# A key transpose placed later in the gate's product, and layer results stored from ScalarE's queue

## The chip, the cores and the metric

One Trainium2 chip, one of its cores. The metric is the device time of one execution in microseconds (us); lower is better. The kernel is built with a tile framework: the program emits instructions, a scheduler orders them on each engine, and helper calls force an order where the author wants one.

## The reference

One layer of a bidirectional encoder is applied to two request groups (prompt and sample), each 2048 tokens of width 1024, in fp32, with shared weights:

```python
h = rms_norm(x, norm_w)
q_a, k_a, v_a, g_a, q_b, k_b, v_b, g_b = split(h @ w_in)      # 512 128 128 512 512 512 512 512
q_a, k_a = rope(rms_norm(q_a)), rope(rms_norm(k_a))            # 8 query heads, 2 key heads of 64
o_a = windowed_gqa_sink(q_a, k_a, v_a, sink_a) * silu(g_a)     # +-128 tokens
o_b = neighbourhood_attn(rms_norm(q_b), rms_norm(k_b), v_b, rpb_b) * silu(g_b)   # 2-D window 8 x 16
x = x + concat([o_a, o_b]) @ w_out
y = x + (p @ w_ple) * sigmoid(x @ w_ple_gate)                  # p: 256 wide per token
```

## The kernel before

Every large product is done in fp32 precision by splitting both operands into a high and a low part and adding three matmuls for each block of 128 rows of the contraction: high by high, high by low, low by high.

**The start.** `proj_a(f)` makes group A's projections for one tile of 128 tokens (f = 0 to 31, two groups of 16 tiles): 24 matmuls of `pk` (keys and values), 24 of `pq` (queries), 24 of `pg` (gates), each 24 being 8 blocks k by 3. The first two tiles run interleaved while the weights still arrive: pk for both, pq for both, then pg of tile 0 and pg of tile 1. The gate's weights `wb` are split into their parts by ACT (L151) and DVE (L152) while PE already runs. The keys are normalised on DVE, rotated by POOL (L520 writes `kt`), and turned by a transpose on PE in `keys_a` (`pkt`, through the helper at L255), from which ACT and DVE write the two parts of the key matrix `ks_a`. `keys_a` is called behind matmul number `ka` of the run pq-then-pg; `KA = 33` means behind the tenth matmul of pg. Later PE needs the rotated query `q` in the same way (`pqt`).

**The middle.** Group B's projections follow (`proj_b`, `pqk` and `pvg`), interleaved with the attention units: a unit is one block of queries. `unit_b` loads its values `vw` (three tiles of 256 KB, L865), computes scores `scb`, a softmax, transposes the probabilities (`ptb`), copies them into a high part on ACT (`p_t`, L894) and a low part on DVE (L895), and multiplies them with `vw` (`pob`; one matmul for each of the unit's three blocks of keys, so each needs its own `vw`). The next unit's queries are prepared in between: ACT writes `q1b` (L836), DVE `q` (L837), twice each. A table sets the order of these parts against the filling matmuls.

**The last six units** (about 1735 to 1821 us) have no projections left to fill PE's waits. The filler is `ple_ahead(n)`: the layer's own product `p @ w_ple` of a tile of 512 tokens, in eight pieces m of 128 columns. Each piece takes six matmuls (`pple`), then ACT copies the sum to `ev` (L1003), and a DMA of 256 KB stores it to `ple_d`. A piece is stored on SP's queue (L981) once the next has been copied. `load_coming` loads, also on SP's queue, weights for the last stage into the tiles `wa0` to `wb7` (512 KB each, L972, `sp_oa`). n = 0 to 4 run inside the units; n = 5 to 7 follow with `tail=True` (stored directly, L1006), with nothing else beside them. After that comes the last stage (output projection and gate, `acca` and `accc`, L1225), which reads `ple_d` back.

**Queues.** The program gives every DMA one of eight semaphores in turn, DMAHW0 to DMAHW7, whichever engine issues it. A DMA waits at its place in the engine's queue until the one before it on the same semaphore, eight DMAs earlier in the order of emission, has landed. `P(...)` keeps an instruction in program order on its engine; everything else is ordered by the scheduler.

Of the kernel before, what the change touches and what calls it, by code (L numbers as in the profile page):

```python
# [69 lines left out]
KA = 33  # L70
# [30 lines left out]
def emit(ctx, tc, io):  # L101
    nc = tc.nc
# [4 lines left out]
    def ptile(shape, tag, name):  # L107
        tag = PSM.get(tag, tag)
        return pp.tile(shape, F32, tag=tag, name=name, bufs=PSB[tag])
# [49 lines left out]
    P = tc.keep_in_program_order  # L159
# [6 lines left out]
    def flush(key):  # L166
        pump(max((i + 1 for i, (k, _) in enumerate(jobs) if k == key), default=0))
# [83 lines left out]
    def mm(out, lhsT, rhs, start, stop):  # L251
        pinned(nc.tensor.matmul(out, lhsT, rhs, start=start, stop=stop))  # L252
# [216 lines left out]
    last = {2 * NT - 2: 48, 4 * NT - 2: 24, 6 * NT - 2: 24}  # L469
# [14 lines left out]
    def proj_a(f):  # L484
        s, t = divmod(f, NT)
        xr, ms, (ssq, ee) = xt.pop(f), ms_a[:, f:f + 1], stats.pop(f)
        ka = 22 if f in last else KA
        early = 1 < f < 2 * NT - 1
        pk = ptile([128, 256], "pj" if f > 1 else "sc", "pk")
        for i, c in enumerate(project(pk, xr, lambda k, b: wx[:, k, b, :], 112)):  # L490
# [439 lines left out]
    ple_d = [dram.tile([128, KT, TW], F32, tag=f"ple_d{n}", name=f"ple_d{n}") for n in range(len(tiles))]  # L930
    p_st, p_rs, early = {}, {}, {}

    def load_p(n):
        if n < len(tiles):
            s, u = tiles[n]
            p_st[n] = []
            for k in range(2):
                st = main.tile([128, TW], F32, tag="stage", name="p32", bufs=2)
                nc.sync.dma_start(st, io["p_t"][s][128 * k:128 * k + 128, TW * u:TW * u + TW])
                p_st[n].append(st)  # L940

    def split_p(n, later=False):

        t = p_rs[n] = main.tile([128, 2, 2, TW], F32R, tag="xr", name="p_r", bufs=2)

        def job(hi, lo, src):
            nc.scalar.copy(hi, src)
            nc.vector.tensor_tensor(out=lo, in0=src, in1=hi.bitcast(F32), op=ALU.subtract)
        for k, src in enumerate(p_st.pop(n)):
            todo = partial(job, t[:, k, 0], t[:, k, 1], src)  # L950
            if later:
                jobs.append((f"p{n}", todo))
            else:
                todo()
# [13 lines left out]
    def load_coming(n=1):  # L968

        for name, tag, key in coming[:n]:  # L970
            w = main.tile([128, 2, 512], F32R, tag=tag, name=tag, bufs=1)
            nc.sync.dma_start(w.bitcast(F32), parts_d[key])  # L972
            early[name].append(w)
        del coming[:n]

    made = []

    def store_ple(n):

        for dst, ev in made[:n]:  # L980
            nc.sync.dma_start(dst, ev)  # L981
        del made[:n]

    def ple_ahead(n, tail=False):

        load_p(n + 1)
        for m in range(KT):
            if m % 4 == 3 and (n < 3 or m == 3):
                load_coming()
            ps = ptile([128, TW], "pj", "pple")  # L990
            if m == 5 and n + 1 < len(tiles):
                split_p(n + 1)
            flush("p0")
            for k in range(2):
                w, c = early["p"][2 * (m // 4) + k], 128 * (m % 4)
                for i, (a, b) in enumerate(((0, 0), (0, 1), (1, 0))):
                    mm(ps, w[:, a, c:c + 128], p_rs[n][:, k, b], k == 0 and i == 0, k == 1 and i == 2)
                    yield 215
            if tail:
                ev = main.tile([128, TW], F32, tag="s", name="ev", bufs=SB)  # L1000
            else:
                ev = ap.tile([128, TW], F32, tag=("ev", "sq")[m // 2 % 2], name="ev", bufs=3 - m // 2 % 2)
            P(nc.scalar.copy(ev, ps))  # L1003
            store_ple(1)
            if tail:
                nc.sync.dma_start(ple_d[n][:, m], ev)  # L1006
            else:
                made.append((ple_d[n][:, m], ev))

    qs = {}  # L1010

# [4 lines left out]
    def filler(f):  # L1016

        gen = proj_a(f) if f < 2 * NT else proj_b(f)
        for n, (cost, last_one) in enumerate(gen):
            if last_one:  # L1020
                next(gen)
            elif hold[0] > 0:
                hold[0] -= 1
            elif n % step[0] == step[0] - 1:
                pump()
            yield cost
# [22 lines left out]
    def paired(f, n):  # L1049
# [20 lines left out]
        else:  # L1070
            for name in ("a12", "a22"):
                load_early(name)
        w_b[half] = w

    stream = chain(*(paired(f, last[f]) if f in last else filler(f) for f in range(2, 6 * NT) if f - 1 not in last),
                   *(ple_ahead(n) for n in range(AHEAD)))
    drain(stream, 24)
    done = 2
# [38 lines left out]
    with tc.tile_pool(name="c", bufs=1, reuse_waits="tile") as op:  # L1117
# [171 lines left out]

        load_raw(0, 0)  # L1290
        drain(ple_ahead(AHEAD, True))
        load_raw(0, 1)
        drain(ple_ahead(AHEAD + 1, True))
        for _ in range(4):
            load_x()
# [12 lines left out]
        for m in range(7 * len(groups)):  # L1308
            n, i = divmod(m, 7)
# [92 lines left out]
```

## Time and profile before

| | before |
|---|---|
| median of 3 runs | 2472.81 us (2471.73 to 2474.23) |
| profiled execution, its own time | 2471.11 us |
| span of its profile | 2469.3 us |
| PE (matmuls) busy | 2453.1 us, 99% |
| PEld (weight loads) busy | 2074.2 us, 84% |
| DVE, ACT, POOL busy | 1703.8, 1413.5, 856.4 us |
| granted PE clock | 1.00 |

PE is TensorE, ACT ScalarE, DVE VectorE, POOL GpSimd, SP SyncE, which here only issues DMAs. A row of a timeline gives start, duration, engine, line, operation, output and inputs, and in square brackets the idle time ahead of it with the instruction that ended it; "x24" means so many instructions in one row. ACTq and SPq are the DMA issues of these engines.

### The profile page before, as it was taken

The page shows a single profiled execution, that of the slowest core. Times are in us where ns is not written, and L with a number is a line of the kernel's source. Part 1 is how long each engine was busy: PE and PEld are TensorE (multiplying, and loading weights), DVE is VectorE, ACT ScalarE, POOL GpSimd, SP SyncE. Part 2 cuts the span into 40 slices and gives each one's busy share as a digit, 9 for nine tenths or more (in the row PEclk, how much of TensorE's full clock was granted, in tenths as well). Part 3 has the DMA queues.
Part 4 walks back from the last instruction along what each step waited for, and adds up shares of the span by engine and source line. Part 5 has one row for each costly group of instructions (what it writes and reads, how often), then busy time and mean ns, then how long its engine had stood idle before and what let it go on. Part 6 is the DMA issues. An engine that isn't in the chain of part 4 may idle for free.

```text
span 2469.3 us, 40516 instructions
## 1 busy us (share of the span) xinstructions
PE 2453.1 (99%) x13050; PEld 2074.2 (84%) x13050; DVE 1703.8 (69%) x4212; ACT 1413.5 (57%) x3407; POOL 856.4 (35%) x1363
## 2 busy tenths in 40 slices
PE   9999999999999999999999999999999999999999
PEld 8888888888888888888888888888888888888887
DVE  7777777777765666666666666666537655677776
ACT  7777776777664665656655566665763212344433
POOL 4555555555543544454544444443110000000000
PEclk9999999999999999999999999999999999999999
DMA  6332223232255565556955566567977445756765
GB/s 227 122 103 93 95 88 103 95 101 88 95 180 164 169 191 183 183 163 196 313 183 179 173 218 202 193 202 230 311 251 269 156 166 175 270 180 207 251 222 170
DMA packets 243172, 442.01 MB, mean 179 GB/s; under 512 B 27888, under 2 KB 82320, under 8 KB 237712
## 3 DMA queue, kind: packets, MB, share of 16 engines
q1 hardware_dynamic: 242672, 439.42, 54.4%
q8 instruction: 104, 1.70, 0.3%
q14 instruction: 108, 0.88, 0.1%
q10 hardware_dynamic: 288, 0.01, 0.0%
HBM read 309.29 MB, written 134.23 MB: 180 GB/s over the span
## 4 chain that ended last, share of the span: by engine, by line
PE 93%; DVE 2%; DMA 2%; ACT 2%; POOL 1%; issue 0%; SPq 0%; DVEq 0%; ACTq 0%; POOLq 0%
PE acca L1225 14%; PE pvg L252 14%; PE pqk L252 14%; PE accc L1225 10%; PE pg L252 7%; PE pq L252 6%; PE scb L252 4%; PE ptb L255 3%; PE pob L252 3%; PE pk L252 3%; PE po L252 3%; PE pple L252 3%; PE sc L252 3%; PE pt L255 2%; DMA vw<-v_d 1%; PE pktb L255 1%
## 5 line engine op out<-in xcount | busy, mean ns | idle before, releaser
L284 ACT ACTIVATE s<-s,nm 128x320 f32<-128x320 f32 (+6 forms) x512 | 294.4, 576 | 317.8 <-DVE nm L279 198.5
L252 PE MATMUL pvg<-wb,xr 128*128 128x512 f32 x1536 | 461.8, 407 | 0.0
L252 PE MATMUL pqk<-wa,xr 128*128 128x512 f32 x1536 | 443.0, 411 | 0.0
L252 PEld LDWEIGHTS pqk<-wa,xr 128*128 128x128 f32 x1536 | 266.0, 189 | 37.0
L252 PEld LDWEIGHTS pvg<-wb,xr 128*128 128x128 f32 x1536 | 266.7, 189 | 31.2 <-DMA wb<-sp_1wb 0.4
L1207 ACT CAST opd<-raw 128x512 fp32r<-128x512 f32 x224 | 131.5, 619 | 271.2 <-PE acca L1225 118.6
L353 POOL TENSOR_TENSOR xr<-stx,xr 128x512 fp32r<-128x512 f32 x186 | 238.9, 1294 | 100.8 <-ACT xr L352 76.0
L1208 DVE TENSOR_TENSOR opd<-raw,opd 128x512 fp32r<-128x512 f32 x224 | 146.4, 685 | 146.6 <-ACT opd L1207 146.6
L252 PE MATMUL pg<-wb,xr 128*128 128x512 f32 x768 | 233.2, 409 | 1.0 <-DVE vv L510 1.0
L252 PE MATMUL pq<-wa,xr 128*128 128x512 f32 x768 | 219.3, 400 | 0.0
L268 DVE CUSTOM_DVE_ANT_0 s<-scb,bias 128x288 f32<-128x288 f32 (+3 forms) x256 | 142.0, 555 | 104.8 <-PE scb L252 101.5
L137 POOL TENSOR_TENSOR yb<-vrb,power 128x8 f32<-128x8 f32 x64 | 106.4, 1662 | 222.7 <-DVE vrb L783 197.1
L1225 PE MATMUL accc<-opd,wb 128*128 128x512 f32 x768 | 176.7, 389 | 0.0
L1225 PE MATMUL acca<-opd,wa 128*128 128x512 f32 x768 | 175.5, 389 | 0.0
L1225 PE MATMUL acca<-opd,s 128*128 128x512 f32 x768 | 175.4, 389 | 0.0
L1225 PEld LDWEIGHTS acca<-opd,wa 128*128 128x128 f32 x768 | 144.2, 188 | 29.9
L1225 PEld LDWEIGHTS accc<-opd,wb 128*128 128x128 f32 x768 | 144.2, 188 | 29.9
L1225 PEld LDWEIGHTS acca<-opd,s 128*128 128x128 f32 x768 | 144.2, 188 | 29.9
L914 DVE TENSOR_TENSOR otb<-pob,otb 64x512 f32<-64x512 f32 x128 | 88.1, 689 | 114.0 <-ACT otb L913 112.4
L252 PEld LDWEIGHTS pob<-p_t,vw 128*128 128x128 f32 (+2 forms) x832 | 132.5, 189 | 27.6 <-DVE p_t L895 4.6
L252 PEld LDWEIGHTS pq<-wa,xr 128*128 128x128 f32 x768 | 135.1, 189 | 17.3
L711 DVE TENSOR_TENSOR pr<-pt,pr 128x512 fp32r<-128x512 f32 (+2 forms) x248 | 135.6, 549 | 17.3 <-ACT pr L709 14.1
(168 smaller groups left out, 5166.8 us busy)
## 6 DMA issues: line engine op xcount, KB each, us to landing
stx<-x_b SPq DMA_DIRECT2D x128, 256.0 KB
vw<-v_d SPq DMA_DIRECT2D x112, 256.0 KB
stx<-x_a SPq DMA_DIRECT2D x64, 256.0 KB
stn<-x_n SPq DMA_DIRECT2D x64, 256.0 KB
v_d<-vb SPq DMA_DIRECT2D x64, 256.0 KB
ple_d<-ev SPq DMA_DIRECT2D x64, 256.0 KB
xres<-x_r SPq DMA_DIRECT2D x64, 256.0 KB
x_d<-r SPq DMA_DIRECT2D x64, 256.0 KB
```

Of the source, the lines that this page charges most:

```text
L137: nc.gpsimd.tensor_tensor(out=y, in0=v, in1=power.broadcast_to([128, n]), op=ALU.pow)
L252: pinned(nc.tensor.matmul(out, lhsT, rhs, start=start, stop=stop))
L255: pinned(nc.tensor.transpose(out, in_, eye))
L268: nc.vector.tensor_tensor_reduce(out=s, in0=ps[:, :n], in1=bias, scale=1.0, scalar=-3.0e38, op0=ALU.add, op1=ALU.max, accum_out=sm["mx"][: ...
L284: ex = nc.scalar.activation(ss[i], ss[i], AF.Exp, bias=nm[:, i:i + 1], accum_out=den[:, i:i + 1])
L353: low.tensor_tensor(out=lo, in0=raw, in1=hi.bitcast(F32), op=ALU.subtract)
L711: nc.vector.tensor_tensor(out=pr[r, 1, to], in0=pt[r, c], in1=pr[r, 0, to].bitcast(F32), op=ALU.subtract)
L914: nc.vector.tensor_tensor(out=ot[a:a + 64], in0=pq[a:a + 64], in1=ot[a:a + 64], op=ALU.add)
L1207: P(nc.scalar.copy(hi, v))
L1208: P(nc.vector.tensor_tensor(out=lo, in0=v, in1=hi.bitcast(F32), op=ALU.subtract))
L1225: pinned(nc.tensor.matmul(ps, w[k][:, a, c:c + 128], o[:, b], start=i in (0, 1, 4) and k == 0 and j == 0, stop=k == 3 and j == 2, skip_gro ...
```

## The change

Two things change. The first tile's key transpose is called behind matmul 44 in place of 33 of the run pq-then-pg: behind the 21st matmul of pg, eleven later. And every store of a piece of `ple_d` is issued from ACT's queue, directly behind the copy that makes it, in place of SP's; the list of pieces made but not yet stored goes, and all 64 stores have one form.

```diff
     def proj_a(f):
-        ka = 22 if f in last else KA
+        ka = 22 if f in last else 44 if f == 0 else KA
...
-    made = []
-
-    def store_ple(n):
-
-        for dst, ev in made[:n]:
-            nc.sync.dma_start(dst, ev)
-        del made[:n]
-
     def ple_ahead(n, tail=False):
...
             P(nc.scalar.copy(ev, ps))
-            store_ple(1)
-            if tail:
-                nc.sync.dma_start(ple_d[n][:, m], ev)
-            else:
-                made.append((ple_d[n][:, m], ev))
+            P(nc.scalar.dma_start(ple_d[n][:, m], ev))
```

The lines of the copy and the store become L995 and L996. On PE, in the first tile's gate product, the order changes as follows; `wb_114` to `wb_120` are the gate's weights of blocks k = 1 to 7.

```order
 L252 MATMUL pg<-wb_114,xr 128x512 x3
 L252 MATMUL pg<-wb_115,xr 128x512 x3
-L252 MATMUL pg<-wb_116,xr 128x512
-L255 MATMUL pkt<-ident,kt 128x128
-L252 MATMUL pg<-wb_116,xr 128x512 x2
+L252 MATMUL pg<-wb_116,xr 128x512 x3
 L252 MATMUL pg<-wb_117,xr 128x512 x3
 L252 MATMUL pg<-wb_118,xr 128x512 x3
 L252 MATMUL pg<-wb_119,xr 128x512 x3
+L255 MATMUL pkt<-ident,kt 128x128
 L252 MATMUL pg<-wb_120,xr 128x512 x3
```

The transpose moves from the middle of block 3 to the end of block 6, ahead of the last three matmuls of pg.

On SP's queue, at the first of the last six units, this stands before the change; `vw<-v_d_312` are the three value loads of that unit, `wb` the weights of the last stage, `ob_d` an attention result.

```order
L972 DMA wb_22354<-sp_oa_230 128x1024 [waits DMAHW4_49,PE_49]
L981 DMA ple_d_322<-ev 128x512 [waits DMAHW5_49,Activation_49]
L981 DMA ple_d_322<-ev 128x512 [waits DMAHW6_49,Activation_49]
L972 DMA wb_22477<-sp_oa_231 128x1024 [waits DMAHW7_49,PE_49]
L972 DMA wb_22594<-sp_oa_232 128x1024 [waits DMAHW0_49,PE_49]
L865 DMA vw<-v_d_312 128x512 [waits DMAHW1_49,PE_49]
L865 DMA vw<-v_d_312 128x512 [waits DMAHW2_49,PE_49]
L865 DMA vw<-v_d_312 128x512 [waits DMAHW3_49,PE_49]
L981 DMA ple_d_322<-ev 128x512 [waits DMAHW4_49,Activation_49]
L923 DMA ob_d_86<-o_tb 128x2x128 [waits DMAHW5_49,DVE_49]
```

And this on the same queue now:

```order
L972 DMA wb_22355<-sp_oa_230 128x1024 [waits DMAHW3_49,PE_49]
L972 DMA wb_22478<-sp_oa_231 128x1024 [waits DMAHW5_49,PE_49]
L972 DMA wb_22595<-sp_oa_232 128x1024 [waits DMAHW7_49,PE_49]
L972 DMA wb_22690<-sp_oa_233 128x1024 [waits DMAHW1_49,PE_49]
L972 DMA wb_22813<-sp_oa_234 128x1024 [waits DMAHW2_49,PE_49]
L865 DMA vw<-v_d_312 128x512 [waits DMAHW4_49,PE_49]
L865 DMA vw<-v_d_312 128x512 [waits DMAHW5_49,PE_49]
L865 DMA vw<-v_d_312 128x512 [waits DMAHW6_49,DMAHW0_49,PE_49]
L865 DMA vw<-v_d_313 120x512 [waits DMAHW7_49,PE_49]
L923 DMA ob_d_86<-o_tb 128x2x128 [waits DMAHW0_49,DVE_49]
```

The stores are gone from it, and two more weight loads (`sp_oa_233`, `sp_oa_234`), which stood behind the value loads, now stand ahead of them.

On ACT, in the same unit, the order before is this; `q1b` belongs to the next unit's queries, the first `p_t` feeds this unit's first `pob`.

```order
L1003 COPY ev<-pple 128x512 [waits DMAHW0_49,PE_49,Activation_49]
L836 ACTIVATE q1b<-pqtb,wk 64x256 [waits PE_49]
L894 CAST p_t<-ptb 128x368 [waits PE_49]
L1003 COPY ev<-pple 128x512 [waits DMAHW5_49,PE_49,Activation_49]
L836 ACTIVATE q1b<-pqtb,wk 64x256 [waits DVE_49]
L894 CAST p_t<-ptb 128x368 [waits PE_49] x2
L1003 COPY ev<-pple 128x512 [waits DMAHW6_49,PE_49,Activation_49]
```

And now:

```order
L995 COPY ev<-pple 128x512 [waits PE_49]
L836 ACTIVATE q1b<-pqtb,wk 64x256 [waits PE_49]
L996 DMA ple_d_322<-ev 128x512 [waits DMAHW2_49,Activation_49]
L836 ACTIVATE q1b<-pqtb,wk 64x256 [waits DVE_49]
L894 CAST p_t<-ptb 128x368 [waits PE_49]
L995 COPY ev<-pple 128x512 [waits DMAHW6_49,PE_49]
L894 CAST p_t<-ptb 128x368 [waits PE_49]
L996 DMA ple_d_322<-ev 128x512 [waits DMAHW4_49,Activation_49]
L894 CAST p_t<-ptb 128x368 [waits PE_49]
```

The store stands between the two `q1b`, and the first `p_t` behind both; the store's semaphore DMAHW2 is that of the weight load `sp_oa_234` in SP's queue. On DVE the two `q` likewise stand together ahead of the first `p_t` in units one to five, where before the first `p_t` stood between them.

## The prediction

> **What bounds the kernel now.** I read the page's busy times and chain first, then what PE waits for, then the timelines and windows at the two places that the change touches.
>
> ```profile
> PE 2453.1 (99%) x13050; PEld 2074.2 (84%) x13050; DVE 1703.8 (69%) x4212; ACT 1413.5 (57%) x3407; POOL 856.4 (35%) x1363
> PE 93%; DVE 2%; DMA 2%; ACT 2%; POOL 1%; issue 0%; SPq 0%; DVEq 0%; ACTq 0%; POOLq 0%
> ```
>
> PE is busy for 2453.1 of 2469.3 us, and the chain that ended last is PE for 93%. The change takes no matmul away and adds none. So it can only remove some of the 16 us in which PE is idle, or add to them. Which of them it can remove, the waits of PE tell (sum in us, count, longest):
>
> ```profile
> PE pob L252 <- DMA vw<-v_d: 1.8, 5, 0.6
> PE pkt L255 <- POOL kt L520: 1.2, 1, 1.2
> PE pob L252 <- DVE p_t L895: 0.9, 2, 0.6
> ```
>
> The 1.2 us is the transpose that is moved. The other two rows lie in the last six units, where the stores move. Together they are 3.9 us. A measurement of this kernel can tell about 0.2%, that is 4.9 us, from no change. So a gain that could be measured is nearly excluded by these three rows, and the question is what the change adds.
>
> **Part one, the transpose.** The start's timeline:
>
> ```profile
> 25.98 2.73 DVE L152 SCALAR_TENSOR_TENSOR wb<-ws,nw,wb 128x512 fp32r<-128x512 f32 x4
> 27.24 0.26 POOL L520 TENSOR_TENSOR kt<-r 128x32 f32<-128x32 f32 x1
> 27.55 0.33 PE L255 MATMUL pkt<-ident,kt 128*128 128x128 f32 x1 [1.22 <-POOL kt L520]
> 27.64 5.73 PE L252 MATMUL pg<-wb,xr 128*128 128x512 f32 x24
> 31.38 0.25 POOL L520 TENSOR_TENSOR kt<-r 128x32 f32<-128x32 f32 x1
> 33.15 0.46 POOL L520 TENSOR_TENSOR q<-r 128x128 f32<-128x128 f32 x1
> 33.21 0.27 PE L255 MATMUL pkt<-ident,kt 128*128 128x128 f32 x1
> 35.17 0.60 PE L255 MATMUL pqt<-ident,q 128*128 128x128 f32 x4
> ```
>
> PE reaches the transpose at 27.55 - 1.22 = 26.33 and waits for `kt`, which POOL ends at 27.50. A pg matmul takes 5.73/24 = 0.239 us, so eleven of them put the transpose at 26.33 + 2.63 = 28.96: `kt` is there, and 1.22 us go. What is late next? The eleven matmuls now run 1.2 us earlier, and four weight blocks (k = 4 to 7) are still being split on DVE, 0.68 us each, the ends at 26.66, 27.35, 28.03 and 28.71. PE wants them after 2, 5, 8 and 11 matmuls: 26.81, 27.52, 28.24 and 28.96. All four are in time, by 0.15 to 0.25 us. The second tile's transpose moves from 33.21 to 31.99, and its `kt` ends at 31.63. The four query transposes begin at 35.17 + 0.60 less four of about 0.27 (the single transpose's row), that is 34.7, or 33.5 without the wait, and POOL ends `q` at 33.61: level, a miss of 0.1 at most. Of `keys_a`'s followers nothing is due soon (the first scores come after the projections). Term: **-1.2 us** (between -0.8 and -1.22).
>
> **Part two, the stores.** What an issue costs on ACT's queue, the two at the kernel's start show:
>
> ```profile
> 0.72 0.41 ACTq L117 DMA_DIRECT2D nw<-norm_w  x1
> 0.72 0.39 SPq L335 DMA_DIRECT2D stx<-x_a  x1
> 1.16 0.46 ACTq L125 DMA_DIRECT2D wkt<-qk_norms  x1
> L981 SPq DMA_DIRECT2D ple_d<-ev x40: 319/326/1215, 1734.8 to 1819.7; - x40
> 1782.44:1796.12 13.68, 13.62 (x75) 11.33 (x74) 8.19 (x21) 10.45 (x25) 2.44 (x5) 1.00 0.61 204
> ```
>
> On ACT 0.41 and 0.46 us, back to back; on SP the same store took 0.32 in the median and 1.2 at worst. I take 0.42 and keep 1.2 for a rival. In each of the six units some seven stores now stand between ACT's copies and casts: 3 us more on an engine that in the unit of 1782.44 to 1796.12, the last row (length, then PE, PEld, DVE, ACT and POOL busy), was busy for 10.45 of 13.68 us. It fits, but what stands behind an issue is late. The transfers themselves stay; what is around them in the first of the units:
>
> ```profile
> 1745.00:1750.00 5.00, 4.53 (x27) 3.39 (x26) 2.83 (x7) 4.93 (x13) 2.43 (x5) 1.00 1.04 390
> 1742.43 1.30 SPq L865 DMA_DIRECT2D vw<-v_d  x3
> 1743.83 0.38 SPq L981 DMA_DIRECT2D ple_d<-ev  x1
> 1752.84 0.42 SPq L972 DMA_DIRECT2D wb<-sp_oa  x1
> 1743.32 6.36 DMA vw<-v_d
> 1748.53 0.35 PE L252 MATMUL pob<-p_t,vw 128*128 128x256 f32 x1
> 1749.72 0.44 PE L252 MATMUL pob<-p_t,vw 128*128 128x128 f32 x2 [0.26 <-DMA vw<-v_d]
> ```
>
> Of the 5 us window the last columns say that all 16 DMA engines were busy (1.04) and moved 390 GB/s; ACT was busy 4.93 of 5.00 us there. So transfers queue: 256 KB take 0.67 us, 512 KB 1.34. The third value load was issued at 1743.32 and landed 6.36 us later, at 1749.68, and PE waited for it.
>
> The Trainium skill, "DMA: Bandwidth & Descriptors", in its section "Issuing engines are not separate DMA queues", says that DMAs from ScalarE, SyncE and GpSimd run on the same 16 engines and interleave, so that issuing on several queues saves issue time only. By that rule the stores gain no bandwidth on ACT, and the loads that come forward on SP still share the engines with them. The window's 1.04 agrees; the terms below stand on that row alone.
>
> *First unit.* Two weight loads of 512 KB, which before were issued from 1752.84 on, behind the value loads, now stand ahead of them. Without the three value loads (2.0 us) what is ahead had landed at 1747.7; the two loads add 2.7 and a store that now comes early 0.67, so the second weight load lands near 1751.0 and the last value load near 1753.0. ACT is caught too: its store waits for the semaphore of that second weight load, and this stands ahead of the first `p_t`:
>
> ```profile
> 1747.20 0.45 ACT L894 CAST p_t<-ptb 128x368 fp32r<-128x368 f32 x1
> 1747.74 0.52 DVE L895 TENSOR_TENSOR p_t<-ptb,p_t 128x368 fp32r<-128x368 f32 x1
> 1748.16 0.47 ACT L836 ACTIVATE q1b<-pqtb,wk 64x256 fp32r<-64x256 f32 x1
> ```
>
> From 1751.0 on: issue 0.42, `q1b` 0.47, `p_t` 0.45, its low part 0.52, together 1752.9. Both ways end near 1753, so the third `pob` goes from 1749.72 to about 1753.2: **+3.5 us**. Ends: 0.9 if the loads ahead have drained by then, 4.2 if another store of 0.67 slips in.
>
> *Second to fifth unit.* Here the issue stands between the two `q1b`, and the first `p_t` behind both, on DVE too:
>
> ```profile
> 1791.47 0.46 DVE L895 TENSOR_TENSOR p_t<-ptb,p_t 128x304 fp32r<-128x304 f32 x1
> 1792.34 0.49 DVE L837 SCALAR_TENSOR_TENSOR q<-pqtb,wk,q1b 64x256 fp32r<-64x256 f32 x1 [0.41 <-ACT q1b L836]
> 1762.26 0.44 DVE L895 TENSOR_TENSOR p_t<-ptb,p_t 120x288 fp32r<-120x288 f32 x1
> 1776.56 0.46 DVE L895 TENSOR_TENSOR p_t<-ptb,p_t 96x304 fp32r<-96x304 f32 x1
> 1804.57 0.46 DVE L895 TENSOR_TENSOR p_t<-ptb,p_t 128x304 fp32r<-128x304 f32 x1
> 1764.17 0.35 PE L252 MATMUL pob<-p_t,vw 120*128 120x256 f32 x1 [0.64 <-DMA vw<-v_d]
> 1777.74 0.28 PE L252 MATMUL pob<-p_t,vw 96*128 96x256 f32 x1
> 1778.43 0.44 PE L252 MATMUL pob<-p_t,vw 96*128 96x224 f32 x2 [0.41 <-DMA vw<-v_d]
> 1791.98 0.56 PE L252 MATMUL pob<-p_t,vw 128*128 128x256 f32 x3
> 1805.46 0.46 PE L252 MATMUL pob<-p_t,vw 128*128 128x256 f32 x3
> 1820.52 0.56 PE L252 MATMUL pob<-p_t,vw 96*128 96x256 f32 x3 [0.57 <-DVE p_t L895]
> ```
>
> In the fourth unit the low part of `p_t` was ready at 1791.93, and `pob` began at 1791.98. With the second `q` ahead of it (to 1792.83) it is ready at 1793.29, 1.36 later. I use this 1.36 for all four. Fourth: **+1.3** (0.8 if the second `q1b` comes half a us earlier, since it no longer waits behind a `p_t` and a copy). Fifth: ready at 1805.03 before, 1806.39 now, against 1805.46: **+0.9**. Third: 1778.38 against a first `pob` at 1777.74; but the 0.41 wait on `vw` behind it goes, since the value loads come earlier on the emptied queue: **+0.3** (0 to 0.6). Second: 1764.06 against 1764.17, where PE waited 0.64 for `vw`; that wait goes, and a short one behind it, with the value loads in time: **-0.4** (-0.9 to +0.3). *Sixth unit*, no `q1b`: `pob` already waited 0.57 for `p_t`, and one or two issues on ACT ahead of the cast add 0.4 or 0.8: **+0.6**.
>
> *The tail.* Behind the units a piece costs ACT this:
>
> ```profile
> 1824.11 0.59 ACT L1003 COPY ev<-pple 128x512 f32<-128x512 f32 x1 [0.77 <-PE pple L252]
> ```
>
> 0.59 copying and 0.77 waiting for PE, 1.36 us a piece; an issue of 0.42 fits into the 0.77. **0**; only an issue of over 0.77 would uncover it.
>
> **Sum.** -1.2 + 3.5 - 0.4 + 0.3 + 1.3 + 0.9 + 0.6 = **+5.0 us**. Against the profiled execution's 2471.11 that is 2476.1; the median of the runs shown is 1.7 above it, so 2477.8.
>
> **The rivals.** (A) is the sum; its own range is +2 to +8, 2474.8 to 2480.8.
>
> (B) *ACT becomes the bound in the six units.* An issue costs nearer 1.2 us (the worst row of SP) than 0.42, or more stores are caught by a semaphore behind loads, as in the first unit. For it: ACT was busy 4.93 of 5.00 us in the window of the first unit, so it has no slack where the stores now stand. Against it: in the median the same issue took 0.33. With 0.8 more for the one issue ahead of the first `p_t` in each of six units: +5.0 + 4.8, about 2482.6.
>
> (C) *The weight loads are through in time.* If what is ahead of the value loads has drained, the first unit pays only ACT's order, 0.9 in place of 3.5: +2.4, 2475.2. For it: five weight loads leave early, one behind the other, without stores between them. Against it: the DMA engines were full all through that window.
>
> (D) *No slower: SP's queue was the trouble.* Without stores ahead of them the value loads land sooner, all five waits on `vw` go (-1.8), the transpose's goes (-1.2), and ACT's issues fall into gaps: -3.0, 2469.8. It decides where a `vw` lands before `pob` and the first `p_t`'s low part is ready by 0.05 us later than before at most (the fourth unit's slack). Against it: the second `q` alone, 0.49, uses that up. That the change does nothing is no case: both orders are altered.
>
> The rows at 0.72 us show ACT and SP issuing at the same time, in 0.41 and 0.39 us, no longer than ACT's next issue (0.46). The Trainium skill, "Perfetto Trace Analysis", in its section "DMA Instruction — HWDGE (DVE, Sync)", says that the block which generates descriptors is shared by two sequencers, and that waiting for its lock counts into the issue. If that holds for ACT and SP, an issue on ACT is stretched while SP issues too, and the time goes towards (B)'s; the two rows speak against much of it.
>
> **How the numbers follow.** (A) 0.48, (B) 0.26, (C) 0.16, (D) 0.10. The time is that of (A), 2477.8. The range leaves out (D) and the far part of (B): 2473.8 to 2485, where the upper end lets one more unit be caught as the first is (2482.6 + 2.4). Slower by over 0.2% means above 2477.8: half of (A), all of (B) and little else, 0.52. Faster by over 0.2% means below 2467.8; only removing all 3.9 us of waits and more would do, 0.03. Within it 0.45.
>
> **What would show it.** In the changed kernel's trace PE should not wait at the first `pkt`, and pg's 24 matmuls run through. In the first of the six units `pob` should wait about 3.5 us, for `vw` or for `p_t`, with an ACT issue standing until a `wb` load lands. In the fourth and fifth units `pob` should wait about 1 us on `p_t` of DVE. In the tail ACT's copies should still wait for PE. I am wrong if PE waits for `vw` nowhere and for `p_t` under 1 us in all, or if ACT's issues take about 1 us each.

## The result, and the profile after

The changed kernel takes 2485.32 us in the median of 4 runs (2484.24 to 2488.2), against 2472.66 us of the kernel before (4 runs): 12.7 us more, a ratio of 1.0055 (95% interval 1.0043 to 1.0067). The prediction had the direction, slower; the size was 5.0 us in the sum, and the measured time lies 0.3 us above the upper end of the range, 2485.0.

The profiled execution took 2485.60 us, 14.5 more than that of before. Its busy times, and the waits of PE (sum, count, longest):

```profile
PE 2457.2 (99%) x13050; PEld 2075.3 (84%) x13050; DVE 1703.2 (69%) x4212; ACT 1414.5 (57%) x3407; POOL 857.2 (35%) x1363
PE pob L252 <- DVE p_t L895: 7.9, 7, 3.5
PE pple L252 <- ACT ev L995: 5.5, 4, 3.5
PE pob L252 <- DMA vw<-v_d: 0.2, 1, 0.2
PE pqt L255 <- POOL q L520: 0.2, 1, 0.2
```

The same 13050 matmuls keep PE busy 4.1 us longer than before (2457.2 against 2453.1), and PE is idle 10.4 us longer (26.6 against 16.2). Together that is the whole difference between the two executions. The wait at `pkt` is gone and `pqt` waits 0.2; the waits on `vw` shrank from 1.8 to 0.2 us; those on `p_t` grew from 0.9 to 7.9; and a row is new, `pple` waiting for `ev`, which the prediction had put at nothing.

The first unit on PE, ACT and SP:

```profile
1751.05 0.49 PE L252 MATMUL pob<-p_t,vw 128*128 128x256 f32 x2 [3.47 <-DVE p_t L895]
1749.06 0.33 ACTq L996 DMA_DIRECT2D ple_d<-ev  x1
1749.43 0.47 ACT L836 ACTIVATE q1b<-pqtb,wk 64x256 fp32r<-64x256 f32 x1 [2.32 <-DMA wb<-sp_oa]
1735.04 6.10 SPq L972 DMA_DIRECT2D wb<-sp_oa  x5
1741.24 5.01 SPq L865 DMA_DIRECT2D vw<-v_d  x4
```

Five weight loads go out ahead of the value loads; ACT's store stands until one of those loads (`wb<-sp_oa`) lands, and the second `q1b` behind it comes 2.32 us late. PE waits 3.47 us. What follows is in windows; the third column from the end is the granted clock:

```profile
1754.00:1755.00 1.00, 1.00 (x4) 0.81 (x4) 0.27 (x1) 0.47 (x1) 0.00 (x0) 0.50 1.01 384
1751.50:1752.25 0.75, 0.56 (x4) 0.52 (x4) 0.75 (x2) 0.73 (x2) 0.00 (x0) 1.00 1.13 368
1752.25:1755.75 3.50, 3.50 (x13) 2.87 (x12) 1.30 (x3) 1.75 (x4) 0.00 (x0) 0.51 1.01 386
1755.75:1756.50 0.75, 0.75 (x6) 0.67 (x6) 0.28 (x1) 0.73 (x2) 0.00 (x0) 1.00 0.54 199
1865.00:1866.00 1.00, 1.00 (x4) 0.81 (x3) 0.66 (x1) 0.00 (x0) 0.00 (x0) 0.50 1.06 402
```

PE's clock is halved for about 3.5 us behind the wait (0.51 in the window of 3.50 us, 1.00 ahead of it and behind it). Half the work of that time is lost, some 1.7 us; a second such stretch lies at 1865. The two make 3.4 of the 4.1 us that PE is busy longer; the other 0.7 is not traced. In the four units behind, `pob` waits for `p_t`:

```profile
1767.87 0.57 PE L252 MATMUL pob<-p_t,vw 120*128 120x256 f32 x3 [0.78 <-DVE p_t L895]
1781.77 0.56 PE L252 MATMUL pob<-p_t,vw 96*128 96x256 f32 x3 [0.65 <-DVE p_t L895]
1796.56 0.56 PE L252 MATMUL pob<-p_t,vw 128*128 128x256 f32 x3 [1.17 <-DVE p_t L895]
1811.21 0.56 PE L252 MATMUL pob<-p_t,vw 128*128 128x256 f32 x3 [1.02 <-DVE p_t L895]
```

The tail, on PE, on ACT, and one link of the chain of waits in order of time (start, length):

```profile
1858.74 1.66 PE L252 MATMUL pple<-p_r,wa 128*128 128x512 f32 x6 [0.73 <-ACT ev L995]
1863.90 4.60 PE L252 MATMUL pple<-p_r,wa 128*128 128x512 f32 x12 [3.50 <-ACT ev L995]
1858.10 0.58 ACT L995 COPY ev<-pple 128x512 f32<-128x512 f32 x1 [1.85 <-PE pple L252]
1860.82 0.33 ACTq L996 DMA_DIRECT2D ple_d<-ev  x1
1851.42 9.32 DMA s<-sums
```

ACT's copy ends at 1858.68, but its store is issued only at 1860.82, when a load of the last stage, `s<-sums`, has landed at 1860.74 on the semaphore that the store waits for. The four casts and the copies that stand behind the store come late, PE waits 3.5 us, and the clock halves for the second time. The loads themselves also come sooner among the stores. The four loads `xres`, on SP's queue, began to go out behind 16 of the tail's 24 stores before (first row), and behind 8 of them now (second row):

```profile
1844.24 2.02 SPq L1244 DMA_DIRECT2D xres<-x_r  x4
1841.38 3.90 SPq L1232 DMA_DIRECT2D xres<-x_r  x4
```

### The profile page after: what moved, and what is told of

It reads as the page before. It is cut to its first block, busy times and chain, and to the rows that moved or that the text cites. A ratio compares the mean times of both kernels' runs of the same rounds, so it can differ in the third digit from the quotient of the medians.

```text
span 2483.8 us, 40478 instructions
## 1 busy us (share of the span) xinstructions
PE 2457.2 (99%) x13050; PEld 2075.3 (84%) x13050; DVE 1703.2 (69%) x4212; ACT 1414.5 (57%) x3407; POOL 857.2 (35%) x1363
## 4 chain that ended last, share of the span: by engine, by line
PE 90%; DVE 3%; DMA 3%; ACT 2%; issue 1%; POOL 1%; SPq 0%; ACTq 0%; DVEq 0%
PE pvg L252 14%; PE pqk L252 14%; PE acca L1213 13%; PE accc L1213 10%; PE pq L252 6%; PE pg L252 6%; PE scb L252 3%; PE ptb L255 3%; PE pob L252 3%; PE po L252 3%; PE pk L252 3%; PE sc L252 3%; PE pt L255 2%; PE pple L252 2%; DVE pr L711 1%
```

## The experiments

Each kernel was measured in rounds with the kernel before on the same chip; the differences are of those medians. Rows of a kernel's waits are sum, count, longest, of one profiled execution each.

**The two parts, and the two halves of the stores.** First the transpose alone:

```diff
-        ka = 22 if f in last else KA
+        ka = 22 if f in last else 44 if f == 0 else KA
```

> Only the transpose moves; the stores stay on SP's queue. All theories agree: PE's wait of 1.22 us at the first pkt goes and a wait of about 0.2 us at the first pqt comes, so the start ends 1.1 us earlier and nothing else changes: 1.1 us (0.04%) less than before, too little for the times, to be read in the waits of PE. If the times show more than 3 us, the transpose has an effect that the traces have not shown.

2471.11 against 2471.95 us, ratio 0.9993 (0.9984 to 1.0002): no difference that the times can tell. The start in its trace:

```profile
29.09 0.27 PE L255 MATMUL pkt<-ident,kt 128*128 128x128 f32 x1
34.46 0.66 PE L255 MATMUL pqt<-ident,q 128*128 128x128 f32 x4 [0.16 <-POOL q L520]
```

No wait at `pkt`, 0.16 at `pqt`: 1.06 us, as expected. All kernels below have the transpose moved. With it in place, only the 24 stores of the tail go to ACT:

```diff
             if tail:
-                nc.sync.dma_start(ple_d[n][:, m], ev)
+                P(nc.scalar.dma_start(ple_d[n][:, m], ev))
```

> Transpose moved; the 40 stores of the six units stay on SP's queue as before, the 24 of the tail go to ACT's. Theory (a store on ACT waits at its place for a semaphore that a load on SP's queue used before it, and holds up the copies behind it): PE waits for ev in the tail for 4 to 6 us, the longest wait over 2 us is followed by a stretch at half clock that costs up to 1.7 us, and no wait is added in the six units: 4 to 6 us more than before. Rival one (ACT is short of issue time): 24 issues of 0.33 us fit into ACT's idle time of 0.77 us a piece, PE waits for ev under 1 us: 0 to 1 us less than before. Rival two (the order of loads in the units, and full DMA engines there): the same, 0 to 1 us less.

2480.72 us, 8.8 more than before (ratio 1.0036, 1.0024 to 1.0049).

```profile
PE pple L252 <- ACT ev L1003: 6.2, 4, 4.1
```

The wait for `ev` is there with these 24 stores alone, and rivals one and two fall for the tail. The size was expected too small (4 to 6 us). The other way round, the 40 stores of the units on ACT's queue and the tail's on SP's:

> Transpose moved; the 40 stores of the six units go to ACT's queue, the 24 of the tail stay on SP's. Theory: the wait of about 3.5 us in the first unit with its half clock (1.7 us) and the waits of 0.7 to 1.2 us for p_t in the four units behind stay, the tail's waits for ev go: about 5.5 to 6 us more than before, 7 us less than with all stores on ACT. Rival one (issue time on ACT): nearly the whole 12.7 us stay. Rival two (order of loads): the first unit's 5 us stay, the four waits for p_t too; it agrees with the theory here and parts from it where the stores go to a third queue.

2479.53 us, 7.6 more (ratio 1.0028, 1.0018 to 1.0038).

```profile
PE pob L252 <- DVE p_t L895: 8.6, 8, 3.7
PE pple L252 <- ACT ev L995: 0.4, 1, 0.4
```

The first unit's wait and the four waits for `p_t` stay, the tail's go. The time lies 1.6 us above what was expected. The halves do not add up: 8.8 and 7.6 are 16.4, the whole is 12.7. In the trace with the tail's stores PE waited longer for `vw` than the 1.8 us of before, though the instructions of these units stand as before:

```profile
PE pob L252 <- DMA vw<-v_d: 4.1, 7, 1.3
```

The clock also halved twice in these units, at a loss of 1.7 us each. This execution took 2484.67 us, 4 us above the median of its kernel, so part of what it shows is not in every execution; the transpose alone, with the same instructions there, showed 2.6 us. Why these waits vary is open.

**The first unit: the loads or ACT's queue?** All stores go to POOL's queue, which has semaphores of its own; SP's order stays that of the changed kernel, ACT's becomes that of before:

```diff
-            P(nc.scalar.dma_start(ple_d[n][:, m], ev))
+            nc.gpsimd.dma_start(ple_d[n][:, m], ev)
```

> Transpose moved; all 64 stores go to POOL's queue, which has semaphores of its own; SP's queue keeps the order of the changed kernel, with two weight loads ahead of the first unit's value loads, and ACT has the order of before. Theory (a store in ACT's queue holds up what stands behind it): no p_t is late, the tail does not wait; what is left in the first unit is the wait for vw behind the two weight loads, 1 to 2.5 us, with or without a short stretch of half clock: 0 to 3 us more than before. Rival one (issue time on ACT): every wait goes, 1 us less than before. Rival two (order of loads and full DMA engines): the first unit still waits for 3 us or more and its clock halves: 4 to 5 us more than before.

2480.17 us, 8.2 more (ratio 1.0033, 1.0022 to 1.0044); the theory as it then stood was wrong, and rival two holds for the first unit.

```profile
1749.05 0.35 PE L252 MATMUL pob<-p_t,vw 128*128 128x256 f32 x1 [2.49 <-DMA vw<-v_d]
1749.96 0.37 PE L252 MATMUL pob<-p_t,vw 128*128 128x224 f32 x1 [0.56 <-DMA vw<-v_d]
1751.23 0.69 PE L252 MATMUL pob<-p_t,vw 128*128 128x128 f32 x2 [0.90 <-DMA vw<-v_d]
PE pple L252 <- ACT ev L995: 2.9, 5, 0.9
```

With no store on ACT the first unit still waits 3.95 us, now directly for the value loads behind the weight loads, and its clock halves behind the wait (0.50 from 1752 to 1754). So the order of the loads suffices there. In the four units behind, no `p_t` is late. The tail still loses 2.9 us, though ACT issues no store. Next, all stores on ACT as in the changed kernel, but value loads kept ahead of weight loads:

```diff
-            nc.sync.dma_start(w.bitcast(F32), parts_d[key])
+            P(nc.sync.dma_start(w.bitcast(F32), parts_d[key]))
...
-                nc.sync.dma_start(v[:kc]...)
+                ld = nc.sync.dma_start(v[:kc]...)
+                if f >= 6 * NT - 6:
+                    P(ld)
```

> The changed kernel, with the loads on SP's queue kept in the order in which the program emits them, so that the first unit's value loads go ahead of four of the five weight loads. Theory (the weight loads ahead of the value loads are what the first unit waits for, directly or through ACT's store on the same semaphore): the wait of 3.5 us in the first unit falls under 1.2 us and its clock stays full, 3 to 5 us less than the changed kernel; the waits for p_t of 0.7 to 1.2 us in the units behind, and the tail's, stay: 7 to 10 us more than before. Rival (a store on ACT's queue is late by itself, whatever loads stand around it): nothing changes, 12 to 13 us more than before.

2480.30 us, 7.6 more than before (ratio 1.0032, 1.0019 to 1.0044), within what was expected.

```profile
1750.34 0.67 PE L252 MATMUL pob<-p_t,vw 128*128 128x256 f32 x4 [0.98 <-DVE p_t L897]
1747.83 0.33 ACTq L998 DMA_DIRECT2D ple_d<-ev  x1
1748.72 0.47 ACT L836 ACTIVATE q1b<-pqtb,wk 64x256 fp32r<-64x256 f32 x1 [0.54 <-DVE q L837]
```

The same store now goes out right behind the first `q1b`; of 3.47 us 0.98 are left. The store's issue is not on that path: it was over at 1748.16, and the second `q1b` waited until 1748.72 for DVE's first `q`. Before, the first `p_t` stood in this gap; now it stands behind it. The 0.98 us are the price of the order on ACT and DVE alone, and the units behind show the same (in the fourth unit of the changed kernel the issue is over at 1794.45, and the second `q1b` waits for `q` until 1795.00). The clock stays full here.

**The half clock.** The wait is filled with matmuls that nobody reads:

```diff
+            if f == 6 * NT - 6 and x == 0:
+                w = early["p"][0]
+                for _ in range(14):
+                    mm(po.rearrange("p i c -> p (i c)"), w[:, 0, :128], w[:, 1], True, True)
```

> The changed kernel, with 14 matmuls that nobody reads (3.35 us at full clock) put where PE waits 3.47 us in the first unit; they write into the PSUM tile that the next product starts afresh. Theory (the clock halves because PE idled): the clock stays 1.00 behind the first unit, what PE computes there takes 1.7 us less, and the whole is 1.5 to 2 us faster than the changed kernel, about 11 us more than before; the tail's half clock stays. Rival (the clock falls for another reason, such as full DMA engines): the half clock stays for 3.4 us, the time is that of the changed kernel or up to 1 us more.

```profile
1751.66 0.49 PE L252 MATMUL pob<-p_t,vw 128*128 128x256 f32 x2 [0.54 <-DVE p_t L895]
1754.00:1755.00 1.00, 1.00 (x8) 0.88 (x7) 1.00 (x3) 1.00 (x3) 0.00 (x0) 1.00 1.03 402
1865.00:1866.00 1.00, 1.00 (x4) 0.81 (x3) 0.00 (x0) 0.00 (x0) 0.00 (x0) 0.56 1.06 408
```

With the DMA engines as full (1.03) and the data as late, the clock stays at 1.00 behind the first unit, and eight matmuls run where four ran; it still falls in the tail. So the half clock behind the first unit came from PE's idling, and not from full DMA engines or late data. The times, 2484.23 us (11.5 more than before, ratio 1.0046, 1.0034 to 1.0059), agree with a gain of 1.7 us but cannot tell it from none.

**The tail: semaphores or loads that run ahead?** The last stage's first loads go to POOL's queue, so that stores on ACT share semaphores with none of them; ACT's order is unchanged:

```diff
-                P(nc.sync.dma_start(x, to_load.pop(0)))
+                P(via[0].dma_start(x, to_load.pop(0)))      # POOL until the last stage's loop; raw, s, wa likewise
```

> The changed kernel, with the last stage's first loads (raw, xres, s, wa: those that run beside the tail) issued from POOL's queue, which has semaphores of its own; ACT's order is the same to the instruction, the bytes too, and the last 14 stores of the tail then share a semaphore with no load. Theory (a store on ACT waits for a load that used its semaphore): PE's waits for ev in the tail fall from 5.5 us under 1.5, no half clock there: 5 to 7 us less than the changed kernel, 6 to 8 more than before. Rival (the DMA engines are full, so a store's buffer comes free late, whatever the semaphores): the waits for ev stay at 4 us or more and the time within 2 us of the changed kernel.

2486.62 us, 13.9 more (ratio 1.0052, 1.0040 to 1.0065): not what the theory expected; the rival holds. The trace is of the fastest of its five executions (2483.58):

```profile
PE pple L252 <- ACT ev L995: 4.5, 4, 2.1
1841.53 0.58 ACT L995 COPY ev<-pple 128x512 f32<-128x512 f32 x1 [4.91 <-DMA ple_d<-ev]
```

The stores no longer wait for loads, but the copies wait for their buffers: the stores themselves land late. So the shared semaphores alone, taken away, give nothing back. The mirror: stores on SP's queue as before, the same loads on POOL's:

> The mirror of the run before: all stores on SP's queue as in the kernel before, the transpose moved, and the last stage's first loads (raw, xres, s, wa) on POOL's queue, so that no store stands ahead of them. Theory one (with the stores gone from their queue, the loads run ahead and take the DMA engines from the stores; ACT then waits for ev buffers and PE for ACT): PE waits for ev in the tail, 2 to 5 us, 1 to 7 us more than before. Theory two (the tail's loss comes from stores in ACT's queue that wait for a semaphore used by a load): a store on SP's queue holds up no copy, PE waits for ev under 1 us, the time is within 2 us of before.

2476.16 us, 3.9 more (ratio 1.0017, 1.0007 to 1.0026).

```profile
PE pple L252 <- ACT ev L1003: 3.8, 5, 1.5
```

Theory one: with stores on SP and loads that nothing holds back, PE waits 3.8 us for `ev`. Then the loads were held behind the pieces again, first by small DMAs from `ev`, on SP's queue for the tail, for all pieces, and on POOL's:

```diff
+                P(nc.sync.dma_start(brake[n][:, m], ev[:, :16]))     # 8 KB behind each store
```

> The changed kernel, with a small copy of each tail piece (16 of 512 columns, 8 KB, to memory that nobody reads) stored from SP's queue behind the real store on ACT's, so that SP's loads again wait for ACT's copies as they did before the change. Theory one (the loads run ahead): PE's waits for ev in the tail fall under 1.5 us, no half clock there, 4 to 7 us less than the changed kernel, 6 to 9 more than before. Theory two (ACT's stores wait for semaphores used by loads): the waits for ev stay at 4 us or more, 11 to 14 us more than before.

> The same small copies behind all 64 stores. On SP's queue three weight loads of five still stand ahead of the first unit's value loads as before, and a fourth too. Theory one: the first unit's wait falls from 3.5 us under 2 with or without a half clock, the waits for p_t in the four units behind (0.7 to 1.2 us each) stay, since ACT's order is that of the changed kernel, the tail's go: 3 to 6 us more than before. Theory two: the tail's stay, 8 to 12 us more than before.

> Both cures of the tail at once: the stores stay on ACT's queue as in the changed kernel, the last stage's first loads are issued from POOL's queue (semaphores of its own), and each waits there behind a small copy (8 KB) of the tail's pieces, so that it neither shares a semaphore with a store nor runs ahead of it. If loads that run ahead and shared semaphores together are the tail's loss, PE's waits on ev (of pple and of acca) fall from 5.5 us under 1.5, no half clock there, 6 to 8 us more than before. If they stay at 3 us or more, a third cause is in it, such as ACT's own time for a copy and an issue, or the small copies and POOL's slower issues.

They gave 11.6, 11.1 and 16.4 us more than before (ratios 1.0050, 1.0046, 1.0068). None can tell the theories apart, because the small copies take part in what they should measure. In the first:

```profile
PE pple L252 <- ACT ev L996: 2.1, 3, 1.4
PE acca L1216 <- ACT ev L996: 1.4, 1, 1.4
1870.81 0.59 ACT L996 COPY ev<-pple 128x512 f32<-128x512 f32 x1 [8.24 <-DMA brake<-ev]
```

The waits fell from 5.5 to 3.5 us, but an 8 KB copy queued behind the loads held the next copy up for 8.24 us. The tail's clock stayed full, but at the first unit it was half for 7 us (1750.5 to 1757.5). In the second, PE waited 3.35 us in the first unit, nearly as long as ever, ACT's store there standing until another store had landed:

```profile
1749.24 0.47 ACT L836 ACTIVATE q1b<-pqtb,wk 64x256 fp32r<-64x256 f32 x1 [2.25 <-DMA ple_d<-ev]
```

In the third the waits for `ev` rose to 5.8 us.

So the loads were held without a DMA: POOL reads one column of each piece, and its loads stand behind that:

```diff
+            if tail:
+                P(nc.gpsimd.tensor_copy(seen, ev[:, :1]))
```

> Stores on ACT's queue as in the changed kernel; the last stage's first loads on POOL's queue, each behind one-column copies by POOL of the tail's pieces, so that they come in the order of before (behind the pieces ahead of them), share no semaphore with a store, and no DMA is added. Theory (the tail's loss is loads that run ahead together with semaphores shared with them): PE's waits on ev fall from 5.5 us under 1.5 and no clock halves there: 6 to 8 us more than before. Rival (ACT's issue in itself, copy and store in one queue): the waits stay at 3 us or more, 10 us or more above before.

2479.03 us, 5.8 more than before (ratio 1.0026, 1.0016 to 1.0035).

```profile
PE pple L252 <- ACT ev L996: 0.2, 1, 0.2
```

With the loads in the old order and no semaphore shared, the tail's stores on ACT cost it 0.2 us, and its clock stays full. ACT's own issue is no third cause. What is left of the 5.8 us are the waits of the six units and the half clock behind the first. And with all stores on SP:

> The same loads, held by POOL in the same way, with all stores on SP's queue. Theory (loads that ran ahead cost the 3.8 us of waits on ev that this kernel showed without the hold): the waits fall under 1 us, the time is that of the kernel before within 2 us. Rival (POOL's slower issues, or its separate queue, cost them): the waits stay at 2.5 us or more, 3 to 6 us more than before.

2472.21 us, 1.1 less than before (ratio 0.9996, 0.9986 to 1.0005); no row of `pple` is left among PE's waits. The 3.8 us came from the order of the loads, not from POOL's queue.

**A version that beats both.** The transpose moved, the stores on SP's queue, and the loads in order, as in the diff above:

> The transpose moved, all stores on SP's queue as before, and the loads of the last six units on SP's queue kept in the order of emission, value loads ahead of weight loads. Theory (the value loads are late where loads and stores stand ahead of them): PE's waits for vw, 1.8 to 2.6 us, fall under 0.6, the first pkt's wait is gone: 2 to 3.5 us less than before, about 0.1%. Rival (the weight loads come so late that the last stage waits): PE waits for wb at the start of the last stage, 0 to 5 us more than before.

2470.23 us against 2472.71, ratio 0.9987 (0.9978 to 0.9996): 2.5 us less than before.

```profile
PE pob L252 <- DMA vw<-v_d: 1.3, 2, 0.9
```

The first unit no longer waits; the waits left are in the second and third. That is less of a fall than expected (under 0.6), and a new row, `pvg` waiting 0.6 us for its weights in the middle, takes some of it back. The interval stays below 1, but it overlaps that of the transpose alone (0.9984 to 1.0002): that the order of the loads adds to the gain is not shown by the times.

## Why the prediction was right or wrong

**The transpose** was right: -1.06 us against -1.2, with the miss of 0.1 at `pqt` that the margin had left open (0.16).

**The first unit** was right in place, cause and size: 3.47 and 0.19 us of waits, and 0.46 at a `ptb`, below, less the 0.48 of before, are 3.6 against 3.5. (The `ptb` is held up in the same way, by a store of ACT that stood until 1742.37 for a weight load.) Both ways named, value loads behind two weight loads and ACT's store on a weight load's semaphore, are real: the second is read in the changed kernel's trace and was not run without the first; the first without the second is the run with stores on POOL (3.95 us), and with the loads in order both go (0.98). The absolute times were not right: ACT's store went out at 1749.06, where the sum had 1751.0, and PE came to the unit's scores 1.75 us sooner than before. The two shifts nearly cancel.

```profile
1744.21 0.66 PE L255 MATMUL ptb<-rowwise,s 128*128 128x128 f32 x4 [0.46 <-ACT s L284]
```

**The second to fifth unit** gave 3.62 us of waits for `p_t` less 1.29 of waits on `vw` that went: 2.3 against a sum of 2.1. In the fourth unit the low part of `p_t` ended 0.86 us after DVE's first `q` began, before; now it ends 2.01 us after it: 1.15 later, where the sum took 1.36. The cause is the one named, `p_t` behind both `q1b` and both `q`; the issue between them costs nothing, as the run with the value loads first showed. The value loads came in time. **The sixth** gave nothing (a wait of 0.53 us in place of 0.57) against 0.6. The other 0.3 us of the row of `p_t` waits lies between 1200 and 1500 us, before and now, and not in the last six units as the prediction has it.

**The tail** is the step that failed: "0; only an issue of over 0.77 would uncover it". The issue does cost less, 0.33 us. But the step priced ACT's time and not what the store waits for, nor what is no longer waited for on SP. In the first unit the prediction had read both from the order of the queues; in the tail, with the same queues and the DMA engines as full, it had not. Measured: 5.5 us of waits for `ev`. The cause that the runs show is the order of the loads: loads of the last stage that no store holds back any more cost 3.8 us alone, and none with the hold. Stores in ACT's queue that stand until such a load lands are seen in the trace (one stood for 2.1 us ahead of the longest wait), but without the shared semaphores 4.5 us were left and the time was no shorter; with both taken away it was 0.2. How much the semaphores add to the loads' order is not settled.

**The clock** was missing from the sum. Two waits of 3.5 us were each followed by about 3.5 us at half clock, 3.4 us lost together. The Trainium skill, "TensorE: Matmul & The Clock Gate", in its section "What's actually happening", says that the clock falls to half after an idle window of about 3.4 us, which runs freely, and comes back after a busy one. The length of the half clock here, 3.5 us, agrees. That a whole window must be idle does not agree: the last section has a clock that fell behind 1.27 us of idle time. By that rule the sum's own wait of 3.5 us, in one piece, could have been followed by one such stretch, an estimate of 1.7 us more.

**The rivals.** (B)'s time, 2482.6, was nearest. Its first reason is not there: an issue on ACT took 0.33 us in the median of 64 and 0.38 at most. Its second, more stores caught by a semaphore behind loads, is seen in the tail, and not in the units that it priced. (C) is not seen, since the first unit waited for the weight loads; its price of ACT's order alone, 0.9, is near the 0.98 of the run with the value loads first. (D) is not seen: the waits on `vw` did go, and ACT's order cost more. The terms that were summed came to 4.8 us against 5.0; what is missing of the 14.5 us between the two traces is 5.5 of the tail, 3.4 of the clock, and the 0.7 that is not traced.

## What to carry to other kernels

A DMA in a queue is also a brake for what stands behind it: taking the stores out of SP's queue let its loads run ahead, and with the DMA engines full (1.06 in the tail's window) the stores landed late. With the stores on SP and the loads let loose, that alone was 3.8 us of waits. Before moving a DMA to a compute engine's queue, read for each one which semaphore it waits for and which transfer used that before, at every place where it will stand, not at one. Read the order of the compute engine too, since the scheduler may change it with the DMAs: here that made waits of 0.7 to 1.2 us in each of four units, where the issue cost nothing. And a wait that leaves PE idle for microseconds is to be priced with the clock that may follow it, 1.7 us or more each time here.

## What was not expected of the hardware

The half clock did not need one long wait. Two kernels with the same instructions at this place (the tail's stores on ACT, and the transpose alone) had nearly the same idle time in the same 2.5 us, and only one lost its clock:

```profile
1747.50:1750.00 2.50, 1.23 (x6) 0.64 (x5) 1.73 (x4) 2.45 (x6) 0.40 (x1) 1.00 1.07 385
1751.00:1754.00 3.00, 3.00 (x12) 2.71 (x11) 0.58 (x2) 1.26 (x3) 0.00 (x0) 0.50 1.00 368
1747.50:1750.00 2.50, 1.17 (x5) 0.42 (x3) 1.59 (x5) 2.45 (x6) 0.40 (x1) 1.00 1.07 369
1751.00:1754.00 3.00, 3.00 (x19) 2.62 (x18) 1.41 (x3) 1.73 (x4) 0.00 (x0) 1.00 0.97 336
```

PE was busy 1.23 of 2.50 us in the first and then ran at 0.50; busy 1.17 in the second, and stayed at 1.00. Nor does one long wait suffice. In the run with all stores on ACT and the value loads first, PE waited 2.89 us in the tail and ran on at 1.00:

```profile
1859.92 3.04 PE L252 MATMUL pple<-p_r,wa 128*128 128x512 f32 x12 [2.89 <-ACT ev L997]
1861.00:1864.00 3.00, 3.00 (x15) 2.47 (x14) 0.69 (x1) 0.59 (x1) 0.00 (x0) 1.00 1.03 363
```

So the length of the wait does not decide alone. Whether the place of a wait within the freely running window named above decides, no run here tests.
